# First feed-forward's output part 1 as seven block products, its modulation rows moved, another offset for v's weights

## The chip, the cores and the metric

The kernel runs on one core of a Trainium2 chip. Times are device microseconds of one execution, from three runs per kernel; a profiled execution gives the trace. The core has a tensor engine (PE; PEld is its weight load), a vector engine (DVE), a scalar engine (ACT), GpSimd (POOL) and SyncE (SP), each with an instruction queue of its own that is worked off in order, and 16 DMA engines that SP's and POOL's issues share. Lower is better.

## The reference, cut to what matters

One decoder block for 512 tokens (T) of width 1024 (D), float32. Nine vectors of 1024 come from `c` by one product with `w_ada`; they shift, scale and gate the three sub-layers.

```
mod = silu(c) @ w_ada + b_ada             # sh1 sc1 gt1 sh2 sc2 gt2 sh3 sc3 gt3
u = modulate(rmsnorm(h, g_norm_ffn1), sh1, sc1)
h = h + 0.5 * gt1 * swiglu(u, w_ffn1_in, w_ffn1_out)     # hidden width 2816
u = modulate(rmsnorm(h, g_norm_mix), sh2, sc2)
h = h + gt2 * token_mixing(u, ...)        # pooling mixer and dilated attention, gated
u = modulate(rmsnorm(h, g_norm_ffn2), sh3, sc3)
h = h + 0.5 * gt3 * swiglu(u, w_ffn2_in, w_ffn2_out)
out = rmsnorm(h, g_final)
```

with `swiglu(u, w_in, w_out) = (silu(a) * b) @ w_out`, where `a, b` are the halves of `u @ w_in`.

## The kernel before

**Precision.** Everything is kept transposed (features on partitions, tokens along the free axis). Each float32 operand is split into a high part, which ACT rounds off (`whi`, line 347), and a low part, which DVE takes as the difference (`wlo`, line 359); each product is three matmuls: high by high, high by low, low by high (`mm3`, lines 391 to 393; `product`, 794 to 796; `out_blocks`, 939 to 941).

**Weights.** They come in chunks of 128 by 1024, in the order of a list that `plan` writes. A chunk is loaded by SP (line 267), then split into a ring of about six and a half chunks. `look(4)` emits the splits of the chunks up to four ahead of the one in use. `room` (line 296) places a chunk at an offset of 0 columns modulo 64, or of 16 (`SHIFT`) for those in `shifted`.

**Plain and block products.** A plain chunk is used in 24 matmuls of 512 columns. Elsewhere a two by two block product is formed from seven products of half-size blocks instead of eight: sums of weight blocks (`make`, line 284, on DVE; two more by accumulating DMAs from POOL, line 292), sums of the data blocks, and 24 matmuls of 256 columns for each of seven chunks. `settle` (line 397) is one extra matmul of 240 columns that stands before such a run where the run before it had 512 columns.

**First feed-forward.** The hidden width is 22 tiles of 128. Tiles 0 to 3 are computed in `startup`, 4 and 5 by `ffn_pair`, and from 6 on two at a time by `duo`, which is a block product of seven steps (i = 0 to 6). The output product is cut in five parts (`PARTS`), each placed after the hidden tiles that it needs and two more: parts 0 and 1 plain, 2 and 3 by `out_blocks` (`BLOCK_PARTS`), 4 plain, as the tail. In this order: pairs 4 and 5, part 0, duos 6 and 8, part 1, duos 10 and 12, part 2, duos 14 and 16, part 3, duos 18 and 20, part 4. For a block part the hidden tiles must be combined too: `block_hidden` gives four differences and sums on DVE, and two high and two low parts. `later(n, f)` puts off work by n steps, so that it is emitted behind the splits of that step.

**Banks.** The eight PSUM banks go round by `nb`. `out_blocks` hands them on in the order C, B, A: the duo behind it starts in C[0], which holds output tiles 0 and 1 until `lower(C, 0)` has added them to H on DVE (line 920, emitted at step i = 4).

**Modulation rows.** `mod` is built from 72 rows of `w_ada`, each one DMA (line 410) of 512 KB and one DVE instruction over 1024 columns (line 418) with an accumulated sum. `bg` does the next row and asks for the one after it; from part 0 on the rows alternate between two buffers, `cs` and `AR`. Rows 24 to 44 stand beside the first feed-forward: eight beside part 1 (two of them `later`), four in duo 8 and four in duo 18 (i = 1, 3, 5, 6), five in duo 20 (i = 0 to 4), by the table `ROWS`. The mixer's norm needs rows 24 to 39.

**Mixer's start.** `head` runs the first four projections (q and k of group 0) beside the second half of the norm. Then `rope_a` sends a copy of them across partitions by 16 DMAs on SP (line 1219), and v of group 0 is computed with the token block as the stationary operand and 256 columns of weights as the moving one (lines 1475 to 1477), four blocks of 24 matmuls. Between them stand `rope_b` (lines 1227, 1228) and three rows. Attention scores (line 1265) follow inside the next tile.

**Angles.** `trig` loads the positions by four small DMAs on SP (line 1177) and does 13 short steps, one behind each tile of part 1 and each step of part 2.

Of the kernel before, what the change touches and what calls it, by code (L numbers as in the profile page):

```python
# [11 lines left out]
AF = mybir.ActivationFunctionType  # L12
# [3 lines left out]
T = 512  # L16
# [118 lines left out]
SHIFT = 16  # L135

PLAIN = {0: 6, 2: 4}
PARTS = ((0, 4), (4, 8), (8, 12), (12, 16), (16, 22))
BLOCK_PARTS = {0: (2, 3), 2: (0, 1, 2, 3)}
ROWS = {8: (1, 3, 5, 6), 18: (1, 3, 5, 6), 20: range(5)}  # L140
NH = 6

MERGED = (6, 7, 0, 1, 2, 3, 4, 5)
# [16 lines left out]
class Kernel:  # L160
# [6 lines left out]
    def plan(self):  # L167
# [40 lines left out]
        def shift(i):  # L208

            self.shifted.update(range(len(self.order) - i, len(self.order)))  # L210
# [23 lines left out]
        base = len(self.order)  # L234
# [3 lines left out]
            plain(mx[i + 4:i + 6])  # L238
        plain(mx[-KT:])
        self.shifted.update(range(base, base + 4))  # L240
        shift(3)
        ffn(2, f2i, f2o, 0)
        shift(5)
# [54 lines left out]
    def room(self, i, held):  # L298


        w, u, at, pieces = self.order[i][0], self.unit(i), self.top, []
        shift = SHIFT if i in self.shifted else 0
        at += (shift - at) % 64
        for c in range(0, w, u):
            if at % RING + u > RING:
                at += RING - at % RING + shift
            o = at % RING
            if pieces and pieces[-1][0] + pieces[-1][1].stop - pieces[-1][1].start == o:
                pieces[-1] = (pieces[-1][0], slice(pieces[-1][1].start, c + u))
            else:  # L310
                pieces.append((o, slice(c, c + u)))
            at += u
        low = min((self.start[j] for j in range(held, i)), default=self.top)
        return (pieces, at) if at - low <= RING else None
# [399 lines left out]

    def ffn_post(self, j, s, pb):
        nc = self.nc
        h = self.wk["hf"][:, j % 2 * T:(j % 2 + 1) * T] if self.n else self.work(("hf", "u3")[j % 2], T)
        nc.vector.tensor_tensor(h, s, pb, op=OP.mult)
        if self.n:
            return  # L720
        hh, hl = self.HH[j % NH], self.HL[j % NH]
        nc.scalar.activation(hh, h, AF.Copy)
        nc.vector.tensor_tensor(hl, h, hh, op=OP.subtract)
# [240 lines left out]
    def ffn2(self):  # L964
        self.put, self.now = [], 0
        self.negate(2)
        bk = [self.nb() for _ in range(4)]
        adds, (s2, s1, s0, last) = self.u_steps(2)
        self.head(2, bk, AF.Silu, adds[:3])
        self.todo = [s0[0], adds[3], s0[1], s2[0], adds[4], s2[1], s1[0], adds[5], s1[1]]  # L970
        do = lambda n: [self.todo.pop(0)() for _ in range(n)]
        for j in range(2):
            self.ffn_post(j, self.ffn_silu(j, bk[2 * j]), bk[2 * j + 1])
            do(2)
        late = self.block_hidden(0)
        pa = self.ffn_tile()
        do(3)
        [f() for f in late[:4]]
        do(len(self.todo))
        self.more()  # L980
        [f() for f in late[4:]]
        s, pb = self.ffn_silu(2, pa), self.ffn_tile()
        self.ffn_post(2, s, pb)
        self.ffn_pair(3)
        late = self.block_hidden(2)
        for i, f in zip((1, 1, 1, 1, 3, 3, 4, 4), late):
            self.later(i, f)
        self.ffn(2, 4, lambda: [f() for f in last])

    def negate(self, n):  # L990
        self.minus = self.mod[:, 0:4]
# [31 lines left out]
    def ffn(self, n, j, last=None):  # L1023
# [10 lines left out]
        for part, (k0, k1) in enumerate(PARTS):  # L1034
            tail = part + 1 == len(PARTS)
            extra = 0 if part and part - 1 in BLOCK_PARTS[n] else 1
            while j < pairs_before(n, part):
                if j < PLAIN[n]:
                    self.ffn_pair(j, beside)
                    j += 1  # L1040
                else:
                    self.duo(n, j, last, tail and j + 2 == FT, extra)
                    last, extra = None, 0
                    j += 2
            if n == 0:
                last = self.beside_out(part) or last
# [5 lines left out]
            if not tail:  # L1052
                for m in range(0, KT, 2):
                    self.look(4)
                    w = self.take()
# [56 lines left out]
    def beside_out(self, part):  # L1112

        if part == 0:

            assert not self.adat
            self.ada_pool.close()
            self.ada_free, self.ada_stop = [self.cs, self.AR], 45
            self.bg_fetch()
            self.negate(0)  # L1120
            self.sums = self.open_sums()
            self.todo, last = self.splits[:3], self.splits[3]
            self.ready = False
            self.todo.append(self.more)
            return last
        if part == len(PARTS) - 1:
            assert self.ada_next == 45 and not self.adat, self.ada_next
            self.ada_free = None
            self.retired = self.rawx
            self.free = [b for b in self.free if not any(b is x for x in self.rawx)]  # L1130
            assert not self.todo
            self.trig_spread()
        if part == 1:
            self.todo = self.trig()
# [281 lines left out]
    def mix(self):  # L1416
# [12 lines left out]
        with tc.tile_pool(name="rt", bufs=1) as self.rt, tc.tile_pool(name="aw", bufs=2) as self.aw, \  # L1429
# [15 lines left out]
            nc.sync.dma_start(self.wpool, self.a["wpool"])  # L1445

            bk = [self.nb() for _ in range(4)]
            self.head(1, bk, AF.Exp)

            uf = mp.tile([P, D], F32, name="uc")  # L1450
            self.ada_free, self.ada_stop, self.ada_depth = [self.AR, uf], 58, 2
            self.bg_fetch()

# [11 lines left out]
            w = self.take() + self.take()  # L1465
            self.look(2)
            for n in range(4):
                if n:
                    self.split(self.pos + n - 1)
                    self.fetch()  # L1470
                b = self.nb()
                ts = slice(n * P, n * P + P)
                for k in range(KT):
                    hi, lo = w[k]
                    M(b[:, :256], self.UH[k][:, ts], hi, start=k == 0, stop=False)
                    M(b[:, :256], self.UH[k][:, ts], lo, start=False, stop=False)
                    M(b[:, :256], self.UL[k][:, ts], hi, start=False, stop=k == KT - 1)
                nc.scalar.activation(self.v1[:, n, :], b[:, :256], AF.Copy)
                for i in ((), (0, 1), (2,), (3,))[n]:
                    self.rope_b(*to[i], 1, sw[i])  # L1480
                if n == 1:

                    self.ada_free += [self.v23.rearrange("p n f -> p (n f)")[:, i * D:(i + 1) * D] for i in range(2)]
                if n:
                    self.bg()
                if n == 2:
                    self.ada_free = [t for t in self.ada_free if t is not uf]
# [20 lines left out]
            for g in (1, 2):  # L1508
                for dst in (self.qt[g], self.kt[g]):
                    for hp in range(2):  # L1510
                        b = self.mm_tile(hooks(todo.pop(0), rest + [(7, self.bg)]))
# [15 lines left out]
            b = self.mm_tile(hooks([], rest + [(3, self.bg), (6, lambda: by_class(0)), (7, self.bg)]))  # L1527
# [6 lines left out]
            def half(i):  # L1534
                if not v4:
# [3 lines left out]
            sums, last = self.mix_sums(x + [self.qt[2]], [[wide(ma, "k2"), wide(mp, "uc")],  # L1539
                                       [wide(ma, "v1"), wide(ma, "k0")], [lambda: half(0), lambda: half(1)]])  # L1540
# [427 lines left out]
```

## Time and profile before

| | us |
|---|---|
| median of 3 runs (lowest, highest) | 974.65 (973.73, 975.48) |
| the profiled execution | 975.12 |
| its span in the trace | 973.0 |
| part 1, with its extra matmul behind it (141.02 to 162.91) | 21.89 |
| part 2 (201.00 to 220.04) | 19.04 |
| part 3 (258.12 to 277.17) | 19.05 |
| v of group 0 (372.79 to 384.30) | 11.51 |

The stretches run from the start of a stage's first matmul to the start of the next stage's first one. The mean granted clock of the tensor engine is 0.999. A time in brackets in a row of the timeline is how long the engine stood idle before the instruction, and what ended that; a row with xN merges N instructions.

### The profile page before, as it was taken

The numbers are of one execution on the slowest core, as the hardware profiler recorded it, in microseconds if no ns is written. First come the engines' busy times: TensorE is split into PE (matmuls) and PEld (weight loads), VectorE is DVE, ScalarE is ACT, GpSimd is POOL, SyncE is SP. The second block draws the span as 40 slices with busy tenths as digits, with TensorE's granted clock in tenths as the row PEclk, the third lists the DMA queues.
The fourth block names the chain that finished last, engine by engine and source line by source line (L and its number), as shares of the span: only waits on it lengthen the run. The fifth ranks groups of instructions, "written<-read, shape, count | busy, mean of one in ns | idle before, by whom it ended". The sixth has DMA issues, their size and how long they took to land.

```text
span 973.0 us, 17631 instructions
## 1 busy us (share of the span) xinstructions
PE 964.1 (99%) x7115; PEld 898.8 (92%) x7115; DVE 824.4 (85%) x1190; ACT 524.8 (54%) x784; POOL 69.7 (7%) x77
## 2 busy tenths in 40 slices
PE   9999999999999999999999999999999999999997
PEld 7888998999999899878879998998999999999997
DVE  7989989999899776898888877889899888989663
ACT  5443553674755453445645553465666657555553
POOL 0000100101010000006300000000101100110002
PEclk9999999999999999999999999999999999999999
DMA  9857777776668525665143327713757666666512
GB/s 351 281 179 254 203 250 217 222 200 155 180 166 266 167 58 183 222 191 179 40 141 109 108 66 224 251 51 111 188 149 187 168 169 173 165 161 153 162 33 87
DMA packets 51507, 165.94 MB, mean 171 GB/s; under 512 B 7009, under 2 KB 9825, under 8 KB 51426
## 3 DMA queue, kind: packets, MB, share of 16 engines
q1 hardware_dynamic: 44224, 140.18, 44.2%
q0 software_dynamic: 6624, 24.12, 14.0%
q8 instruction: 55, 0.90, 0.4%
q10 hardware_dynamic: 578, 0.53, 0.2%
q14 instruction: 26, 0.21, 0.1%
HBM read 135.29 MB, written 2.24 MB: 141 GB/s over the span
## 4 chain that ended last, share of the span: by engine, by line
PE 94%; DVE 3%; issue 1%; DMA 1%; ACT 1%; POOL 0%; POOLq 0%; SPq 0%; DVEq 0%
PE bank L796 13%; PE bank L795 13%; PE bank L794 13%; PE bank L391 11%; PE bank L392 11%; PE bank L393 11%; PE bank L941 4%; PE bank L940 4%; PE bank L939 4%; PE bank L1894 2%; PE bank L1896 1%; PE bank L1898 1%; PE bank L1563 1%; PE bank L1265 1%; PE bank L1316 1%
## 5 line engine op out<-in xcount | busy, mean ns | idle before, releaser
L359 DVE TENSOR_TENSOR wlo<-raw,whi 128x1024 fp32r<-128x1024 f32 (+3 forms) x156 | 169.2, 1095 | 40.9 <-ACT whi L347 40.7
L794 PE MATMUL bank<-UH,whi 128*128 128x256 f32 x640 | 176.7, 276 | 0.0
L795 PE MATMUL bank<-UL,whi 128*128 128x256 f32 x640 | 176.7, 276 | 0.0
L796 PE MATMUL bank<-UH,wlo 128*128 128x256 f32 x640 | 176.7, 276 | 0.0
L359 DVE TENSOR_TENSOR wlo<-X,whi 128x1024 fp32r<-128x1024 f32 (+3 forms) x123 | 135.6, 1112 | 22.6 <-ACT whi L347 22.0
L347 ACT ACTIVATE whi<-raw 128x1024 fp32r<-128x1024 f32 (+3 forms) x156 | 143.9, 938 | 18.2 <-DVE raw L284 10.5
L347 ACT ACTIVATE whi<-X 128x1024 fp32r<-128x1024 f32 (+3 forms) x123 | 117.1, 969 | 22.4 <-DVE X L284 17.0
L794 PEld LDWEIGHTS bank<-UH,whi 128*128 128x128 f32 x640 | 120.1, 188 | 0.2
L795 PEld LDWEIGHTS bank<-UL,whi 128*128 128x128 f32 x640 | 120.1, 188 | 0.0
L796 PEld LDWEIGHTS bank<-UH,wlo 128*128 128x128 f32 x640 | 120.1, 188 | 0.0
L796 PE MATMUL bank<-SH,wlo 128*128 128x256 f32 x408 | 112.6, 276 | 0.0
L794 PE MATMUL bank<-SH,whi 128*128 128x256 f32 x408 | 112.6, 276 | 0.0
L795 PE MATMUL bank<-SL,whi 128*128 128x256 f32 x408 | 112.6, 276 | 0.0
L391 PE MATMUL bank<-UH,whi 128*128 128x512 f32 (+1 forms) x304 | 105.9, 348 | 0.0
L392 PE MATMUL bank<-UL,whi 128*128 128x512 f32 (+1 forms) x304 | 104.5, 344 | 0.0
L393 PE MATMUL bank<-UH,wlo 128*128 128x512 f32 (+1 forms) x304 | 104.3, 343 | 0.0
L795 PEld LDWEIGHTS bank<-SL,whi 128*128 128x128 f32 x408 | 76.6, 188 | 0.0
L796 PEld LDWEIGHTS bank<-SH,wlo 128*128 128x128 f32 x408 | 76.6, 188 | 0.0
L794 PEld LDWEIGHTS bank<-SH,whi 128*128 128x128 f32 x408 | 76.6, 188 | 0.0
L391 PE MATMUL bank<-HI,whi 128*128 128x512 f32 (+1 forms) x214 | 71.5, 334 | 0.0
L392 PE MATMUL bank<-HK,whi 128*128 128x512 f32 (+1 forms) x214 | 71.1, 332 | 0.0
L393 PE MATMUL bank<-HI,wlo 128*128 128x512 f32 (+1 forms) x214 | 71.1, 332 | 0.0
(373 smaller groups left out, 2290.8 us busy)
## 6 DMA issues: line engine op xcount, KB each, us to landing
raw<-wmix SPq DMA_DIRECT2D x44, 512.0 KB, 3.9
raw<-wf1i SPq DMA_DIRECT2D x32, 512.0 KB, 4.8
raw<-wf2i SPq DMA_DIRECT2D x30, 512.0 KB, 4.3
ada<-wada SPq DMA_DIRECT2D x23, 512.0 KB, 5.6
X<-raw POOLq DMA_DIRECT2D x22, 512.0 KB, 5.3
AR<-wada SPq DMA_DIRECT2D x17, 512.0 KB, 4.5
X<-wf2i SPq DMA_DIRECT2D x14, 512.0 KB, 4.8
cs<-wada SPq DMA_DIRECT2D x11, 512.0 KB, 4.4
```

The source lines that it names most:

```text
L347: self.nc.scalar.activation(self.hi[:, y], r[:, x], AF.Copy)
L359: self.nc.vector.tensor_tensor(self.lo[:, y], r[:, x], self.hi[:, y], op=OP.subtract)
L391: M(ps, hi, uh, start=start, stop=False)
L392: M(ps, hi, ul, start=False, stop=False)
L393: M(ps, lo, uh, start=False, stop=stop)
L794: M(o, hi, uh, start=start and p == 0 and k == 0, stop=False, skip_group_check=True)
L795: M(o, hi, ul, start=False, stop=False, skip_group_check=True)
L796: M(o, lo, uh, start=False, stop=k == 3, skip_group_check=True)
L939: M(o, hi, uh, start=start and m % 2 == 0 and k == 0, stop=False, skip_group_check=True)
L940: M(o, hi, ul, start=False, stop=False, skip_group_check=True)
L941: M(o, lo, uh, start=False, stop=k == 1, skip_group_check=True)
L1894: M(b, hi, self.UH[k], start=k == 0, stop=False)
```

## The change

Part 1 of the first feed-forward's output is done by `out_blocks`. Its hidden tiles 4 and 5, which come from plain pairs, are therefore kept whole (`ffn_post` returns early for them) and combined by `block_later`, emitted beside part 0. The rows are placed anew: none beside part 1; i = 3 and 6 in duos 8, 12 and 16; five in duo 18; five in duo 20; and five (40 to 44) in the mixer's `head`, with buffers `uc`, `q1`, `k1` and then `AR`. The two chunks of v's weights get offset 48, and a `settle` matmul stands before v's first block.

```diff
-BLOCK_PARTS = {0: (2, 3), 2: (0, 1, 2, 3)}
-ROWS = {8: (1, 3, 5, 6), 18: (1, 3, 5, 6), 20: range(5)}
+BLOCK_PARTS = {0: (1, 2, 3), 2: (0, 1, 2, 3)}
+ROWS = {8: (3, 6), 12: (3, 6), 16: (3, 6), 18: (0, 1, 3, 5, 6), 20: range(5)}
...
         self.shifted.update(range(base, base + 4))
+        self.beside = range(base + 4, base + 6)
...
-        shift = SHIFT if i in self.shifted else 0
+        shift = 3 * SHIFT if i in self.beside else SHIFT if i in self.shifted else 0
...
-        h = self.wk["hf"][:, j % 2 * T:(j % 2 + 1) * T] if self.n else self.work(("hf", "u3")[j % 2], T)
+        whole = j >= PLAIN[0] - 2 or self.n
+        h = self.wk["hf"][:, j % 2 * T:(j % 2 + 1) * T] if whole else self.work(("hf", "u3")[j % 2], T)
         nc.vector.tensor_tensor(h, s, pb, op=OP.mult)
-        if self.n:
+        if whole:
             return
...
-        late = self.block_hidden(2)
-        for i, f in zip((1, 1, 1, 1, 3, 3, 4, 4), late):
-            self.later(i, f)
+        self.block_later(2)
         self.ffn(2, 4, lambda: [f() for f in last])
+
+    def block_later(self, j):
+        for i, f in zip((1, 1, 1, 1, 3, 3, 4, 4), self.block_hidden(j)):
+            self.later(i, f)
...
                     self.ffn_pair(j, beside)
                     j += 1
+                    if j == PLAIN[0]:
+                        self.block_later(j - 2)
...
-            self.ada_free, self.ada_stop = [self.cs, self.AR], 45
+            self.ada_free, self.ada_stop = [self.cs, self.AR], 40
...
-            self.head(1, bk, AF.Exp)
-
             uf = mp.tile([P, D], F32, name="uc")
+            self.ada_free, self.ada_stop, self.ada_depth = [uf, self.qt[1], self.kt[1]], 45, 3
+            self.bg_fetch()
+            self.ada_free.append(self.AR)
+            self.head(1, bk, AF.Exp, [self.bg] * 5)
+            assert self.ada_next == 45 and not self.adat, self.ada_next
             self.ada_free, self.ada_stop, self.ada_depth = [self.AR, uf], 58, 2
             self.bg_fetch()
...
                 ts = slice(n * P, n * P + P)
+                if n == 0:
+                    self.settle(b, self.UH[0][:, ts], w[0][0])
                 for k in range(KT):
```

More of the change, by code (lines that the diff above doesn't have):

```diff
@@ L984, in ffn2 @@
         self.ffn_pair(3)
-        late = self.block_hidden(2)
-        for i, f in zip((1, 1, 1, 1, 3, 3, 4, 4), late):
+        self.block_later(2)
+        self.ffn(2, 4, lambda: [f() for f in last])
+    def block_later(self, j):
+        for i, f in zip((1, 1, 1, 1, 3, 3, 4, 4), self.block_hidden(j)):
             self.later(i, f)
-        self.ffn(2, 4, lambda: [f() for f in last])
     def negate(self, n):
@@ L1126, in beside_out @@
         if part == len(PARTS) - 1:
-            assert self.ada_next == 45 and not self.adat, self.ada_next
+            assert self.ada_next == 40 and not self.adat, self.ada_next
             self.ada_free = None
```

## The prediction

> **What bounds the kernel.** I read the page's engine shares, then the chain that ended last, then the busy time of each engine stage by stage.
>
> ```profile
> PE 964.1 (99%) x7115; PEld 898.8 (92%) x7115; DVE 824.4 (85%) x1190; ACT 524.8 (54%) x784; POOL 69.7 (7%) x77
> PE 94%; DVE 3%; issue 1%; DMA 1%; ACT 1%; POOL 0%; POOLq 0%; SPq 0%; DVEq 0%
> 102.82:141.02 38.20, 38.20 (x339) 38.20 (x337) 32.52 (x38) 23.21 (x32) 2.61 (x3) 1.00 0.81 229
> 141.02:162.91 21.89, 21.89 (x99) 18.13 (x98) 19.94 (x33) 7.36 (x8) 0.87 (x1) 1.00 0.71 219
> 162.91:201.00 38.09, 38.09 (x338) 38.09 (x337) 37.28 (x49) 20.89 (x28) 4.33 (x5) 1.00 0.80 226
> 201.00:220.04 19.04, 19.04 (x170) 19.04 (x169) 17.16 (x24) 15.30 (x24) 0.95 (x2) 1.00 0.75 201
> 258.12:277.17 19.05, 19.05 (x171) 19.05 (x170) 16.06 (x19) 13.58 (x19) 1.72 (x2) 1.00 0.68 168
> 277.17:315.25 38.08, 38.08 (x339) 38.08 (x337) 36.30 (x52) 19.33 (x27) 1.75 (x2) 1.00 0.77 232
> 356.06:372.55 16.49, 16.49 (x142) 16.49 (x141) 8.98 (x18) 6.44 (x12) 0.00 (x0) 1.00 0.37 128
> 372.90:384.30 11.40, 11.40 (x97) 11.40 (x96) 9.26 (x14) 5.60 (x10) 0.00 (x0) 1.00 0.44 97
> ```
>
> In the stretches the columns are length, then PE, PEld, DVE, ACT and POOL busy, clock, DMA share and GB/s. PE is never idle at full clock, so the time is the number of matmuls times their spacing. Two things then decide: what PE no longer does, and whether DVE (83 to 98% busy in the same stretches) stays far enough ahead.
>
> **The change part by part.** *Part 1.* It goes from the 96 wide matmuls and one `settle` of the second stretch (21.89) to 168 narrow ones as in part 2 (19.04, 113.3 ns each): 21.89 − 19.04 = 2.85 us less, settle included, since duo 10 now follows 256-column products as duo 14 does.
>
> *Work for DVE.* A 1024-column instruction holds DVE 1.14 us when packed (312.85 to 314.00 below); shorter ones from these groups (busy, mean ns, idle):
>
> ```profile
> L418 DVE SCALAR_TENSOR_TENSOR cs<-cs,cond 128x1024 f32<-128x1024 f32 x11 | 13.4, 1218 | 0.3 <-DMA cs<-wada 0.3
> L889 DVE TENSOR_TENSOR GK<-wide,GI 128x768 fp32r<-128x768 f32 x4 | 3.8, 953 | 0.0
> L887 DVE SCALAR_TENSOR_TENSOR wide<-wide 128x256 f32<-128x256 f32 x8 | 3.4, 425 | 0.3
> 80.79 0.69 DVE L723 TENSOR_TENSOR HK<-wide,HI 128x512 fp32r<-128x512 f32 x1 [0.70 <-ACT HI L722]
> 90.20 0.69 DVE L723 TENSOR_TENSOR HK<-ev,HI 128x512 fp32r<-128x512 f32 x1 [0.70 <-ACT HI L722]
> 125.73 1.23 DVE L359 TENSOR_TENSOR wlo<-X,whi 128x1024 fp32r<-128x1024 f32 x1 [2.32 <-ACT whi L347]
> 126.88 1.22 DVE L819 TENSOR_TENSOR wide<-wide 128x1024 f32<-128x1024 f32 x1
> 137.14 1.29 DVE L359 TENSOR_TENSOR wlo<-X,whi 128x768 fp32r<-128x768 f32 x2 [1.00 <-ACT whi L347]
> 141.24 1.22 DVE L418 SCALAR_TENSOR_TENSOR AR<-AR,cond 128x1024 f32<-128x1024 f32 x1
> 142.87 1.94 SPq L1177 DMA_DIRECT2D tr<-pos  x4
> 149.03 0.23 DVE L1181 CAST tr<-tr 128x128 f32<-128x128 int32 x1 [1.14 <-DMA tr<-pos]
> 216.76 1.66 DVE L920 SCALAR_TENSOR_TENSOR H<-bank,mod,H 128x256 f32<-128x256 f32 x4
> ```
>
> Beside part 0, `block_hidden(4)` adds 4 × 0.4 + 1.14 + 0.87 = 3.6 us; the two L723 fall away with their waits on ACT, 2 × (0.60 + 0.70) = 2.6, and some 0.3 of waits of the splits behind them. So nothing there, and the 2.32 us idle before 125.73 covers the rest.
>
> From 126.88 on, up to the start of part 1: two rows fewer (−2.3), block sums and G of tiles 6 and 7 (+1.6 + 0.9), two `make` for part 1 (+2.3), less 1 us of idle (137.14): DVE reaches the end of its last row before part 1 some 1.3 us later, at 143.7 instead of 142.4. Behind that row SP sends a row's DMA and then the four of `trig`: 144.2 to 146.1 instead of 142.87 to 144.81. They landed 4.2 us after issue (cast at 149.03), so they bound the cast to 150.3 at the most; DVE itself arrives at 148.3 (one half-width add, a split, a multiply and the four block sums: 0.6 + 1.14 + 1.2 + 1.6). Between the cast and the second update of `lower(C, 0)`, which frees C[0], stand seven 1024-column instructions, GK, five small steps and two updates: 8.0 + 0.9 + 0.8 + 0.8 = 10.5. C[0] is free at 158.8 to 160.8; duo 10 wants it at 141.02 + 19.04 = 160.06. In part 2 this had 2.4 us to spare (216.76 + 0.8 against 220.04). I take 0 for this stall (the lower end, as there are fewer loads in flight than before); its upper end is 2 us, with the scatter of my sum.
>
> *Rows in duos 12 and 16.* One and two more rows; parts 2 and 3 have 1.9 and 3.0 us of idle DVE (19.04 − 17.16, 19.05 − 16.06) to take them: 0.
>
> *Rows in duos 18 and 20.* One more, and the closing steps of row 39 move from duo 18 to the end of duo 20. There DVE's lag does cost:
>
> ```profile
> 297.97 0.17 DVE L429 TENSOR_TENSOR mod<-mod,vecs 128x8 f32<-128x8 f32 x1
> 306.14 0.33 SPq L410 DMA_DIRECT2D AR<-wada  x1
> 310.66 1.23 DVE L418 SCALAR_TENSOR_TENSOR AR<-AR,cond 128x1024 f32<-128x1024 f32 x1 [1.40 <-DMA AR<-wada]
> 312.85 1.23 DVE L418 SCALAR_TENSOR_TENSOR cs<-cs,cond 128x1024 f32<-128x1024 f32 x1
> 314.00 0.95 DVE L359 TENSOR_TENSOR wlo<-raw,whi 128x768 fp32r<-128x768 f32 x1
> 315.45 0.60 ACT L816 ACTIVATE wide<-bank 128x512 f32<-128x512 f32 x1 [2.98 <-PE bank L796]
> 317.13 1.22 DVE L819 TENSOR_TENSOR wide<-wide 128x1024 f32<-128x1024 f32 x1
> 319.48 1.23 DVE L826 TENSOR_TENSOR HK<-wide,HI 128x1024 fp32r<-128x1024 f32 x1 [1.13 <-ACT HI L801]
> 320.94 0.40 PE L392 MATMUL bank<-HK,whi 128*128 128x512 f32 x1
> ```
>
> The last product's silu is ready at 316.05, but DVE multiplies only at 317.13, then come the high part on ACT and the low part, done at 320.7: 0.24 us before PE wants it. The new row at i = 0 of duo 18 puts DVE 1.14 us back, with no idle until the row loads; 0.25 is absorbed there (0.3 idle in the `cs` group above). The 1.40 us of idle before 310.66 absorbs nothing, because that row's load goes out only after the row before in the same buffer (306.14), which is late too. With the closing steps (0.4, lines 429 and 431) the multiply is 0.9 + 0.4 = 1.3 late, so PE waits 1.3 − 0.24 = 1.05. Bounds: 0 if the loads land sooner, 1.6 if DVE gets nothing back. I take 0.9.
>
> *Mixer's head and v.*
>
> ```profile
> AR<-wada SPq DMA_DIRECT2D x17, 512.0 KB, 4.5
> 366.84 0.42 SPq L410 DMA_DIRECT2D uc<-wada  x1
> 366.92 0.48 DVE L529 SCALAR_TENSOR_TENSOR UL<-ev,mod,UH 128x256 fp32r<-128x256 f32 x1 [0.18 <-ACT UH L515]
> 372.70 4.99 SPq L1219 DMA_DIRECT2D q<-v  x8
> 372.71 1.29 DVE L1221 TENSOR_TENSOR q<-bank,cs 128x512 f32<-128x512 f32 x2 [5.31 <-ACT v L1216]
> 377.23 1.22 DVE L359 TENSOR_TENSOR wlo<-raw,whi 128x1024 fp32r<-128x1024 f32 x1 [2.04 <-ACT whi L347]
> 387.70 0.69 DVE L1228 TENSOR_TENSOR k<-k,k 128x512 f32<-128x512 f32 x1
> 387.82 1.12 PE L1265 MATMUL bank<-k,q 64*128 64x128 f32 x8
> ```
>
> One row fits ahead of the norm's last steps, four into the 5.31 us of idle before 372.71 (4 × 1.14 = 4.6). The last waits for a load that can leave only about when uc's left before (366.84) and lands some 4.5 us later (the first row, median), at 371.3, and SP's 16 copies stand behind the next loads into the same buffers. Cost 0 to 1 us; I take 0.1. v's 96 matmuls go from 11.51/96 = 120 ns to perhaps 113.3, less one settle of 0.11: −0.53 of PE. But the scores at 387.82 wait for DVE's last rope step (387.70 + 0.69), and DVE is packed from 377.23, whose start hangs on the end of v's first block, which moves by 0.05 only. I take −0.05; bounds −0.53 and 0.
>
> Sum: −2.85 + 0 + 0 + 0.9 + 0.1 − 0.05 = −1.9 us. Profiled, 975.12 − 1.9 = 973.2; the median of the runs lies 0.47 under the profiled execution: 974.65 − 1.9 = **972.75**, say 972.7.
>
> ```profile
> L939 PEld LDWEIGHTS bank<-HI,whi 128*128 128x128 f32 x192 | 36.0, 188 | 0.0
> ```
>
> A weight load is 188 ns here and yet narrow matmuls follow every 113 ns, so loads are hidden. The Trainium skill, page "TensorE: Matmul & The Clock Gate", section "Back-to-back issue gap", gives sustained spacings of about 81 ns at 128 columns and 131 at 512, where a load and matmul pair has a large fixed share. By its line an estimate for 256 is 98, and part 1 would go from 96 × 131 = 12.6 to 168 × 98 = 16.4, 3.8 us slower. The trace disagrees (227 and 113 ns, near proportional).
>
> **The rivals.** *All covers hold (A).* The tail's row loads land early and DVE keeps up: −2.85 − 0.05, 971.7. For: 4 us landings vary by a microsecond or two, and one microsecond suffices. Against: the fixed order of buffers.
>
> *C[0] is late too (B).* The bank computed above comes 0.5 to 2 us late: 973.2 to 974.7, centre 974. For: DVE's demand in duos 6, 8 and part 1 is about their length. Against: 2.4 us spare in part 2.
>
> *A stall that leaves PE out of step, slower (C).* The place is duo 10's first product, the price a slower spacing of everything behind it. In the head, after a wait, 140 matmuls of 256 took 16.49 us (117.8 ns each) with nothing to set them right. If C[0] comes after 160.06 and the same step sets in, six duos and two parts (8 × 168 = 1344 matmuls) lose 4.5 ns each, 6.0 us, since no settle stands there any more: 972.7 + 0.5 + 6.0 = 979, or 976 and up if the step comes back midway. Against: it needs B first, and parts 2 and 3 run without it.
>
> *Loads not hidden (D).* If each narrow matmul took its load's 188 ns, part 1 would last 168 × 0.188 = 31.6, +9.7: 984. Parts 2 and 3 speak against it. The Trainium skill's rule quoted above leans towards it.
>
> *v does nothing.* The offset leaves 120 ns: the time is the forecast's within 0.1, as DVE sets that point.
>
> **How the numbers follow.** Forecast (972.2 to 973.2, v's case within it) 0.43, A 0.27, B 0.17, C 0.11, D 0.02. 0.2% of 974.65 is 1.95 us, about what can be told from no change. Faster (under 972.7): A 0.27 and some 0.17 of the forecast, 0.44. Slower (over 976.6): C, D and a remainder of the stalls adding up, 0.15. Within: 0.41. The range leaves out C and D and a little of A: 971.3 to 975.2; the forecast's own is 972.2 to 973.2.
>
> **What would show it.** Part 1 at 19.04 from first matmul to duo 10's first (more is B); spacing in duos 10 to 20 at 113.3 (118 is C); no gap at the second half of the tail's first two tiles, HK ready before PE's L392 (a gap is the 0.9); v's stretch near 11.0, and the wait among the eight scores longer by as much. I am wrong if part 1 saves less than 2.8, or if PE waits in places not named, such as part 0 or the norm's second half.

## The result, and the profile after

The changed kernel takes 981.27 us (median of 9 runs, 975.76 to 982.87) against 974.93 (9 runs, 973.73 to 976.57): a ratio of 1.0057, 95% interval 1.0035 to 1.0078. It is slower by 6.3 us, where 972.7 was forecast. Its runs also lie much further apart than those of before: 7 us against 3. The profiled execution is one of the shortest, 976.68 us (span 974.9); it shows a first part of the loss (its span is 1.9 us longer than before), and the other runs must hold more.

The page of the profiled execution, engine shares and then the chain that ended last:

```profile
PE 961.5 (99%) x7187; PEld 898.8 (92%) x7187; DVE 838.2 (86%) x1222; ACT 534.3 (55%) x806; POOL 70.3 (7%) x79
...
PE 82%; DVE 9%; DMA 3%; issue 3%; ACT 1%; SPq 1%; POOL 0%; POOLq 0%; DVEq 0%; ACTq 0%
```

PE is busy 2.6 us less than before, but the chain now runs 9% through DVE and 3% through DMA (before 3% and 1%): there are waits of PE that these end. Where, by stretches (columns as in the prediction: part 1; duos 10 and 12; duos 14 to 20 with part 3; the tail; v):

```profile
141.29:160.33 19.04, 19.04 (x170) 19.04 (x169) 17.95 (x29) 13.36 (x19) 1.12 (x2) 1.00 0.77 212
160.33:198.85 38.52, 38.36 (x338) 38.16 (x337) 36.38 (x48) 21.90 (x29) 3.57 (x5) 1.00 0.64 166
217.89:313.09 95.20, 95.20 (x842) 95.20 (x841) 90.12 (x117) 54.92 (x75) 7.78 (x9) 1.00 0.74 209
313.09:331.78 18.69, 16.95 (x74) 13.44 (x73) 14.74 (x21) 8.48 (x12) 0.00 (x0) 1.00 0.51 145
372.42:383.31 10.89, 10.89 (x99) 10.89 (x97) 8.02 (x12) 5.54 (x9) 0.00 (x0) 1.00 0.59 174
```

Part 1 is 19.04, as forecast. The next stretch is 0.43 longer than 38.09, and the tail is 18.69 where before it is 16.39:

```profile
315.25:331.64 16.39, 16.39 (x74) 13.51 (x73) 12.46 (x15) 8.48 (x12) 0.00 (x0) 1.00 0.50 142
```

By the starts of the same matmuls in the two traces (v after by its new settle), the difference after − before runs like this:

| at the start of | before | after | difference | change |
|---|---|---|---|---|
| pairs | 59.30 | 59.57 | +0.27 | |
| duo 10 | 162.91 | 160.33 | −2.58 | −2.85 |
| part 2 | 201.00 | 198.85 | −2.15 | +0.43 |
| tail | 315.25 | 313.09 | −2.16 | −0.01 |
| settle behind the tail | 331.64 | 331.78 | +0.14 | +2.30 |
| v | 372.79 | 372.30 | −0.49 | −0.63 |
| mixer tile behind v | 384.30 | 383.31 | −0.99 | −0.50 |
| last scores of that tile | 388.45 | 388.89 | +0.44 | +1.43 |
| second settle in front of the last norm | 941.74 | 943.05 | +1.31 | +0.87 |
| end of the span | 973.0 | 974.9 | +1.9 | +0.6 |

The 0.43 in duo 12, in the timeline of ACT and PE:

```profile
181.60 1.06 ACT L348 ACTIVATE whi<-raw 128x1024 fp32r<-128x1024 f32 x1 [1.43 <-DMA raw<-X]
...
189.93 0.59 ACT L803 ACTIVATE ev<-bank 128x512 f32<-128x512 f32 x1
...
190.57 0.39 PE L796 MATMUL bank<-SH,whi 128*128 128x256 f32 x1 [0.16 <-ACT ev L803]
```

ACT stands idle until an accumulating DMA of POOL has landed; everything behind that split in its queue is late, last the copy that hands a bank back to PE. POOL issues this DMA only behind a `make` of DVE: 13.98 us after duo 10's first matmul (174.31 − 160.33), where before it was 12.79 (175.70 − 162.91). The 2.30 in the tail:

```profile
310.01 1.23 DVE L419 SCALAR_TENSOR_TENSOR cs<-cs,cond 128x1024 f32<-128x1024 f32 x1 [1.63 <-DMA cs<-wada]
...
312.62 1.23 DVE L419 SCALAR_TENSOR_TENSOR AR<-AR,cond 128x1024 f32<-128x1024 f32 x1 [0.50 <-DMA AR<-wada]
...
317.33 1.23 DVE L821 TENSOR_TENSOR wide<-wide 128x1024 f32<-128x1024 f32 x1
...
318.59 1.06 ACT L803 ACTIVATE HI<-wide 128x1024 fp32r<-128x1024 f32 x1 [4.70 <-DVE wide L821]
...
319.70 0.50 PE L392 MATMUL bank<-HI,whi 128*128 128x512 f32 x1 [0.98 <-ACT HI L803]
...
320.95 0.50 PE L393 MATMUL bank<-HK,whi 128*128 128x512 f32 x1 [0.76 <-DVE HK L828]
```

DVE's multiply (line 821, was 819) starts 4.24 us behind the tail's first matmul; before it was 1.88 (317.13 − 315.25). By the clock it starts at nearly the same time (317.33 against 317.13): PE has come 2.16 us earlier, DVE has not. The last two rows of duo 20 wait 1.63 and 0.50 for their loads, and the closing steps follow. And the 1.43 among the scores:

```profile
371.01 0.33 SPq L411 DMA_DIRECT2D AR<-wada  x1
...
372.16 0.33 SPq L411 DMA_DIRECT2D uc<-wada  x1
...
372.58 6.05 SPq L1225 DMA_DIRECT2D q<-v  x8
...
378.70 0.69 DVE L1233 TENSOR_TENSOR q<-q,cs 128x512 f32<-128x512 f32 x1 [0.76 <-DMA q<-v]
...
381.53 1.22 DVE L419 SCALAR_TENSOR_TENSOR AR<-AR,cond 128x1024 f32<-128x1024 f32 x1
...
385.14 1.22 DVE L419 SCALAR_TENSOR_TENSOR uc<-uc,cond 128x1024 f32<-128x1024 f32 x1
...
388.89 0.49 PE L1271 MATMUL bank<-k,q 64*128 64x128 f32 x4 [1.58 <-DVE k L1234]
```

PE reaches the scores a microsecond earlier than before (386.81 against 387.82; the head runs at 113 ns a matmul in its second half, v at 113), but DVE's rope chain ends 0.4 later than it did: two row loads stand ahead of SP's copies, and DVE waits 0.76 for the first copies. All that PE gained is waited away.

### The profile page after: what moved, and what is told of

Same layout as the page of the kernel before. It is cut to its first block, busy times and chain, and to the rows that moved or that the text cites. A ratio compares the mean times of both kernels' runs of the same rounds, so it can differ in the third digit from the quotient of the medians.

```text
span 974.9 us, 17849 instructions
## 1 busy us (share of the span) xinstructions
PE 961.5 (99%) x7187; PEld 898.8 (92%) x7187; DVE 838.2 (86%) x1222; ACT 534.3 (55%) x806; POOL 70.3 (7%) x79
## 4 chain that ended last, share of the span: by engine, by line
PE 82%; DVE 9%; DMA 3%; issue 3%; ACT 1%; SPq 1%; POOL 0%; POOLq 0%; DVEq 0%; ACTq 0%
PE bank L796 10%; PE bank L798 10%; PE bank L797 10%; PE bank L392 10%; PE bank L393 10%; PE bank L394 10%; PE bank L942 4%; PE bank L941 4%; PE bank L943 4%; DVE wlo L360 3%; PE bank L1905 2%; PE bank L1909 1%; PE bank L1907 1%; DMA AR<-wada 1%; DVE H L922 1%
## 5 line engine op out<-in xcount | busy, mean ns | idle before, releaser
L360 DVE TENSOR_TENSOR wlo<-raw,whi 128x1024 fp32r<-128x1024 f32 (+6 forms) x157 | 170.1, 1094 | 38.1 <-ACT whi L348 38.0
L348 ACT ACTIVATE whi<-raw 128x1024 fp32r<-128x1024 f32 (+6 forms) x157 | 144.1, 934 | 31.9 <-DVE raw L285 10.4
L360 DVE TENSOR_TENSOR wlo<-X,whi 128x1024 fp32r<-128x1024 f32 (+6 forms) x136 | 140.0, 1044 | 17.6 <-ACT whi L348 17.4
L348 ACT ACTIVATE whi<-X 128x1024 fp32r<-128x1024 f32 (+6 forms) x136 | 121.3, 915 | 36.0 <-DVE X L285 29.5
L796 PEld LDWEIGHTS bank<-UH,whi 128*128 128x128 f32 x640 | 120.1, 188 | 0.2
L797 PEld LDWEIGHTS bank<-UL,whi 128*128 128x128 f32 x640 | 120.1, 188 | 0.0
L798 PEld LDWEIGHTS bank<-UH,wlo 128*128 128x128 f32 x640 | 120.1, 188 | 0.0
L392 PEld LDWEIGHTS bank<-UH,whi 128*128 128x128 f32 x304 | 57.1, 188 | 8.6 <-issue 1.9
L394 PEld LDWEIGHTS bank<-UH,wlo 128*128 128x128 f32 x304 | 57.1, 188 | 7.0
L393 PEld LDWEIGHTS bank<-UL,whi 128*128 128x128 f32 x304 | 57.1, 188 | 6.8 <-DVE UL L530 0.3
```

What stands on the lines that cost most here:

```text
L348: self.nc.scalar.activation(self.hi[:, y], r[:, x], AF.Copy)
L360: self.nc.vector.tensor_tensor(self.lo[:, y], r[:, x], self.hi[:, y], op=OP.subtract)
L392: M(ps, hi, uh, start=start, stop=False)
L393: M(ps, hi, ul, start=False, stop=False)
L394: M(ps, lo, uh, start=False, stop=stop)
L796: M(o, hi, uh, start=start and p == 0 and k == 0, stop=False, skip_group_check=True)
```

## The experiments

Lines of diffs are against the changed kernel, if nothing else is said. All of these kernels compute the whole block. PE is called in step where its 256-column matmuls follow each other every 113.3 ns, and out of step where they follow every 117.8; it loses the step when it goes from the first to the second.

**e1: the changed kernel once more.** No edit.

> The changed kernel once more, to catch the profile of an execution that takes 981 to 983 us rather than 976.7. Out of step (rival C): two or more duos between 160 and 313 us show a spacing near 118 ns in place of 113.3, so that the stretch from the first matmul of duo 10 to the tail's first one is 157 to 159 us against 152.8 in the profile of 976.7, while part 1 stays at 19.0. More waits (the rival): the spacing stays at 113.3 and single gaps of PE, of 0.4 us and more, in duos 10 to 20, in the tail and in the mixer add up to the 5 to 6 us.

979.54 us (979.39 to 981.74; before on that chip 974.53), profiled at 979.39. Two places differ from the shorter profile. First duo 10, DVE, ACT and PE:

```profile
164.97 1.28 DVE L931 TENSOR_TENSOR ev<-ev,bank 128x512 f32<-128x512 f32 x2
...
165.74 0.58 ACT L803 ACTIVATE bank<-bank 128x512 f32<-128x512 f32 x1 [2.71 <-DVE ev L931]
...
166.37 0.19 PEld L796 LDWEIGHTS bank<-SH,whi 128*128 128x128 f32 x1 [0.28 <-ACT bank L803]
```

C[0] came 0.1 us late at duo 10's first product, PE then ran 46 matmuls at 118 ns, and at the third product it waited for a second bank: DVE's sums of the block part (line 931) release it. Behind this wait it was in step again, up to the tail, so the lost step cost this execution 0.2 us. Part 1 itself took 19.20 here (141.18 to 160.38): PE waited in its middle too, behind a copy of ACT. Then the tail, PE's timeline and, below it, the busy times of the stretch behind these waits:

```profile
321.02 0.50 PE L392 MATMUL bank<-HI,whi 128*128 128x512 f32 x1 [2.02 <-ACT HI L803]
322.28 0.50 PE L393 MATMUL bank<-HK,whi 128*128 128x512 f32 x1 [0.76 <-DVE HK L828]
```

```profile
322.85:326.50 3.65, 3.65 (x10) 2.81 (x9) 1.86 (x3) 0.63 (x1) 0.00 (x0) 0.53 0.03 11
```

The granted clock of the stretch is 0.53: nine 512-column matmuls take 3.65 us instead of 2.04. So there is a third loss that neither theory had: PE waits, and then runs at half clock, 1.6 us more. This execution lost its time in waits (2.02 and 0.76 in the tail, 2.26 at the scores) and in that stretch.

**e2: a settle ahead of duos 10, 14 and 18.**

```diff
-            extra = 0 if part and part - 1 in BLOCK_PARTS[n] else 1
+            extra = 0 if n and part and part - 1 in BLOCK_PARTS[n] else 1
```

> One settle matmul ahead of duos 10, 14 and 18 (3 x 0.11 us). If the 981 to 983 us come from duos that run out of step behind a block part, all runs fall to 976 to 977. If the step is lost at another place, or the time goes into waits, the median stays at 980 to 982.

980.62 us (978.75 to 984.51): no better. The settle did not keep PE in step, it put it out of step: in its profile the matmuls behind the settle of duo 10 start every 118 ns at once, and after a wait in that duo they stay at 118 up to duo 18. There the third settle found the step again, so such a matmul can do either.

**e3: the row of duo 18 elsewhere.**

```diff
-ROWS = {8: (3, 6), 12: (3, 6), 16: (3, 6), 18: (0, 1, 3, 5, 6), 20: range(5)}
+ROWS = {6: (4,), 8: (3, 6), 12: (3, 6), 16: (3, 6), 18: (1, 3, 5, 6), 20: range(5)}
```

> The row at i = 0 of duo 18 goes to i = 4 of duo 6. If that row is what makes the tail's HK late, the two gaps of the tail (together 2.3 us in the profile of the changed kernel) shrink to 0.2 to 0.5 us and the time falls by about 2 us. If the closing steps behind the last row and its late loads do it, they stay above 1.5 us and the time does not move.

977.21 us (973.45 to 985.04). The tail, in the stretch from its first matmul to the settle:

```profile
317.84:334.59 16.75, 16.69 (x75) 13.44 (x73) 12.86 (x17) 8.49 (x12) 0.00 (x0) 1.00 0.45 136
```

0.36 above before's 16.39, where the changed kernel had 2.30. The median is 2.3 us below e1's on the same chip, with runs from 973 to 985. But this profile lost the step in duo 12 and ran 1078 matmuls at 117.8 ns, 4.9 us: PE came that much later to the tail, which gives DVE time, so the 0.36 is not the row's doing alone. e5 and e8 below both reach the tail in step, e5 (first) with this row and e8 without it:

```profile
312.28:332.57 20.29, 16.91 (x74) 13.45 (x73) 15.21 (x21) 8.56 (x13) 0.00 (x0) 1.00 0.52 157
```

```profile
312.38:329.70 17.32, 16.66 (x74) 13.44 (x73) 13.47 (x17) 8.48 (x12) 0.00 (x0) 1.00 0.48 131
```

So the row makes most of the tail's loss, and 0.93 us stays without it (17.32 − 16.39).

**e4: the kernel before with v's offset and settle alone** (the three edits of the change that concern v).

> The kernel before with v's offset and settle alone. v's 96 matmuls go from 11.5 to 10.9 us. If DVE's rope steps set the scores, as in the prediction, the wait among the scores grows by the same 0.6 and the time stays within 0.1 us of before; if PE sets them, the time falls by 0.5 to 0.6 us. It does not touch the first feed-forward, so its runs should not scatter more than those of before.

975.12 us (973.95 to 976.85), ratio 1.0006 (0.9997 to 1.0016). v is 0.6 shorter, and the last scores start 0.91 us behind the ones in front of them instead of 0.41: DVE sets them, as predicted.

**e5: the angles one part later.**

```diff
-        if part == 1:
+        if part == 2:
             self.todo = self.trig()
```

> The steps of the angles stand beside parts 2 and 3 in place of 1 and 2: some 1.7 us less for DVE (the wait for their DMA and five short steps) ahead of the two releases that duo 10 waits for. If DVE's lag behind part 1 makes PE stumble in duos 10 and 12 and fall out of step there, C[0] and the sums come over a microsecond early, duos 10 to 20 run at 113.3 ns and the time falls by 2 to 4 us, to 976 to 977, with the tail's and the scores' waits left. If the stumbles come from the late accumulating DMA in duo 12 or from elsewhere, the median stays at 979 to 982.

979.73 us (978.94 to 980.05). In the profile duos 10 and 12 take 38.08 us with no gap, so DVE's lag behind part 1 was the cause there (POOL's DMA goes out 12.84 us behind duo 10's first matmul, 172.60 − 159.76, near the 12.79 of the kernel before); but PE then waited 2.62 + 0.76 us in the tail and 2.46 at the scores, with one half-clock stretch: DVE's chain ends no earlier for it (PE goes on in the tail at 320.5, in the two profiles of the changed kernel at 319.7 and 321.0), and what PE gains ahead is waited away. The time was missed for that reason.

**e6: part 1 plain again,** the rest of the change kept, no rows beside part 1.

> Part 1 plain again, and no rows beside it: the new places of the rows, the head's five rows and v's offset remain. If the block product of part 1 is what puts DVE late, there is no stumble in duos 10 and 12, all runs lie together, and part 1 takes 21.9 us again: 2.85 us more than the block part, less the steps lost: 977 to 979. If the rows in duos 8 and 12 do it, the stumbles are still there and the runs scatter from 979 to 985. The tail's gaps and the scores' wait stay in both cases.

979.69 us (979.09 to 981.24). Duos 10 and 12 run without a gap, with the same rows in duos 8 and 12: it is the block product that puts DVE late there. And without any gain in part 1 the rows, the head and v cost 5.1 us by themselves, with no step lost in the profile: waits of 0.66 + 0.77 us in the tail (18.33 long in all, 1.94 more than before), 2.38 at the scores, and a half-clock stretch.

**e7: two rows out of the rope chain.**

```diff
-                if n:
+                if n > 2:
                     self.bg()
-                if n == 2:
-                    self.ada_free = [t for t in self.ada_free if t is not uf]
...
-            self.ada_free, self.ada_stop, self.ada_depth = [self.AR, uf], 58, 2
+            self.ada_free, self.ada_stop, self.ada_depth = [self.AR], 57, 2
...
-                        b = self.mm_tile(hooks(todo.pop(0), rest + [(7, self.bg)]))
+                        b = self.mm_tile(hooks(todo.pop(0), rest + [(2, self.bg)] * (len(todo) == 6) + [(7, self.bg)]))
...
-            beside = [(1, 7, nxt), (2, 2, nxt), (2, 3, clear), (2, 6, self.bg), (2, 7, nxt), (3, 2, self.at_swap), (3, 2, nxt),
+            beside = [(0, 7, self.bg), (1, 7, nxt), (2, 2, nxt), (2, 3, clear), (2, 6, self.bg), (2, 7, nxt), (3, 2, self.at_swap), (3, 2, nxt),
```

> Rows 45 and 46 leave the chain of rope steps beside v for later stages of the mixer (two instructions of 1.14 us, and one load less ahead of SP's copies). If DVE's chain sets the scores, PE's wait of 1.6 to 2.3 us there falls to 0 to 0.4, and with it the half-clock stretch that follows waits of about 2 us: 1.6 to 3.5 us off the median, 976 to 978. If the copies' DMAs set it, the wait falls by no more than 0.5 us.

978.98 us (977.32 to 982.36): the median missed, the mechanism not. The eight scores run without a wait (PE, timeline):

```profile
391.85 0.71 PE L1271 MATMUL bank<-k,q 64*128 64x128 f32 x8
```

But two duos of the first feed-forward take 39.58 us instead of 38.08 (stretch):

```profile
220.32:259.90 39.58, 39.58 (x339) 39.58 (x337) 35.88 (x44) 20.79 (x28) 3.44 (x4) 1.00 0.68 177
```

PE is busy all through at full clock, and each matmul takes 117.8 ns. This execution lost the step at 166 us, at the wait for the second bank (0.37 us in all; C[0] was in time), and kept it lost until the tail: 1294 × 4.5 ns = 5.8 us. Its first feed-forward is that of the changed kernel, line for line.

**e8: e3, e5 and e7 together.**

> The three edits together: angles one part later, the row of duo 18 in duo 6, two rows out of the rope chain. If the three waits are independent, part 1's 2.85 us and some 1 us of v and the head come through: 970 to 971.5, in all runs. If one wait only hands over to another, 973 to 976, and scattered.

973.76 us (971.71 to 978.83; before 974.57), 0.9998 (0.9982 to 1.0014). Between the two theories: no gap between pair 4 and the tail, none at the scores, 0.9 in the tail; but two runs at 978 to 979, and 1.25 us of waiting in the mixer behind the row moved there.

**e9 and e10: more rows moved.** e9 takes the last row of duo 20 to i = 5 of duo 12, and the mixer's row from (0, 7) to (0, 1); e10 also takes a row of duo 8 to pair 5.

> The three edits of before and two more: the last row of duo 20 goes to i = 5 of duo 12, and the row that held up the copy of the third class (PE idle 1.25 us there) goes to the idle stretch ahead of it. If the tail's remaining gap hangs on that row's load, it falls from 0.7 us to 0.2 or less; with the copy on time another 1 us goes: 971 to 972 for the bulk of the runs. If the tail's gap stays, it is the closing steps and the split behind them.

> As e9, and the second row of duo 8 goes ahead of part 0, to pair 5, where DVE has 3 us of idle time: 1.1 us more slack for the two releases that duo 10 waits for. If the runs at 978 in e8 come from a stumble there, all runs lie within 971 to 972.5; if they come from elsewhere, some are still 5 us longer than the rest.

e9: 975.05 us (970.65 to 979.91); e10: 973.96 (971.67 to 975.68; before 974.87), 0.9987 (0.9978 to 0.9997). In both the mixer's wait grew, to 1.84, and the row in duo 12 made part 2's banks late; e9's tail kept its 0.76. e10's profile shows what is left of the scatter, against e8 at the same place in duo 8 (ACT):

```profile
131.18 1.07 ACT L348 ACTIVATE whi<-X 128x1024 fp32r<-128x1024 f32 x1 [2.80 <-DMA X<-raw]
...
133.83 0.57 ACT L803 ACTIVATE ev<-bank 128x512 f32<-128x512 f32 x1
```

```profile
128.32 1.06 ACT L348 ACTIVATE whi<-X 128x1024 fp32r<-128x1024 f32 x1
...
130.98 0.57 ACT L803 ACTIVATE ev<-bank 128x512 f32<-128x512 f32 x1
```

The same accumulating DMA lets the split start 2.9 us later, and the copy that frees PE's bank stands behind it. POOL issued it at nearly the same time in both (122.42 in e8, 122.58 in e10).

**e11: the waits of the changed kernel filled** with matmuls of no use, four in the tail and seven ahead of the scores.

> The changed kernel with idle time of PE filled: four 512-column matmuls of no use in the tail's gap and seven in the wait among the scores, 0.9 and 1.6 us, about what PE waits there at the least. If the half-clock stretches follow from PE standing idle some 2 us, none is left, the granted clock is 0.999 in all runs, and the median falls by 1 to 2 us to 978 to 980. If they have another cause, the clock stays at 0.995 to 0.997 in most runs and the time does not fall.

981.95 us (977.11 to 984.31). No half-clock stretch in its profile (clock 0.998), and other runs had 0.995 and 0.997. On the half clock it is inconclusive; e13 and e14 were made for that. But its profile shows rival C. Up to the tail this kernel is the changed one; C[0] came 0.2 us late at duo 10's first product, and PE was out of step from there to the tail (stretch):

```profile
161.66:320.40 158.74, 158.67 (x1346) 158.47 (x1346) 146.06 (x193) 90.87 (x127) 13.03 (x15) 1.00 0.71 194
```

The changed kernel's profile of 976.68 has 152.76 for this stretch. The 6.0 us between them are the spacing: 1340 × 4.5 ns.

**e12: the kernel before with one settle ahead of duo 14.**

```diff
-                    self.duo(n, j, last, tail and j + 2 == FT, extra)
+                    self.duo(n, j, last, tail and j + 2 == FT, 1 if n == 0 and j == 14 else extra)
```

> The kernel before with one settle matmul ahead of duo 14, where 256-column matmuls follow 256-column ones: no wait, no other work, 0.11 us by itself. If a shift of PE by a part of a matmul is enough to put the pairs of matmul and weight load out of step for good, duo 14 to duo 20 run at 117.8 instead of 113.3 ns: 840 x 4.5 ns = 3.8 us, 978.3. If only a true wait does it, or the step is found again, the time stays at 974.6 to 975.

978.24 us (977.93 to 979.72; before 974.87): to 0.1 us what was expected of the loss of step. Duos 14 and 16, then part 3:

```profile
219.86:259.43 39.57, 39.57 (x339) 39.57 (x337) 35.38 (x44) 20.65 (x28) 4.13 (x5) 1.00 0.66 165
259.43:279.22 19.79, 19.79 (x171) 19.79 (x169) 16.31 (x19) 13.57 (x19) 1.72 (x2) 1.00 0.65 162
```

No engine is late here and PE never stands idle. One matmul of another length is enough, and here nothing sets PE right until 512-column matmuls come.

**e13 and e14: the kernel before with one or two DVE instructions of no use in the rope chain** (one in the diff; two in its place in e14).

```diff
+                for _ in range(1 if n == 3 else 0):
+                    nc.vector.tensor_tensor(self.ev[:, :D], self.ev[:, D:], self.ev[:, D:], op=OP.add)
                 for i in ((), (0, 1), (2,), (3,))[n]:
```

> The kernel before with one DVE instruction of 1.14 us and of no use in the rope chain ahead of the scores, so that PE's wait there grows from 0.4 to about 1.5 us. If the half-clock stretch needs about 2 us of idle time, none comes: the time rises by 1.1 us, to 975.9, and the granted clock stays at 0.998 to 0.999. If any wait of PE over 1 us brings it on, the time rises by 2.7 us.

> Two such instructions: a wait of about 2.7 us. If standing idle for more than 2 us halves PE's clock for one stretch of 3.4 us, the time rises by 2.3 + 1.7 = 4.0 us, to 978.8, the clock falls to 0.997, and the trace shows some eight 512-column matmuls of 427 ns behind the wait. If the half-clock stretches of the changed kernel had another cause, it rises by 2.3 us, to 977.1, at 0.999.

e13: 975.98 us (975.35 to 976.94), clock 0.998 to 0.999 in all ten runs. e14: 977.10 (976.84 to 978.75), and here the two theories share the runs: three at 976.8 to 977.1 with clock 0.999, two at 978.4 and 978.8 with 0.997 and 0.996. One of these was profiled; e13's wait, then e14's wait, and the stretch behind e14's:

```profile
389.47 0.49 PE L1265 MATMUL bank<-k,q 64*128 64x128 f32 x4 [1.27 <-DVE k L1228]
```

```profile
390.48 0.56 PE L1265 MATMUL bank<-k,q 64*128 64x128 f32 x4 [2.53 <-DVE k L1228]
```

```profile
390.97:394.39 3.42, 3.42 (x11) 2.70 (x9) 3.32 (x15) 0.83 (x5) 0.00 (x0) 0.53 0.92 316
```

So a wait of 2.5 us brings the half clock on in some executions, at 1.6 us each, and one of 1.3 in none.

**e15: the rest of DVE's work out of the way.** As e10, with the row of duo 12 in pair 5 too and the mixer's row in the third gate tile.

> As e10, with the row of duo 12 in pair 5 as well and the last row of the mixer's classes in the third gate tile, away from GpSimd's work. If DVE's lag and its collision with GpSimd were what the earlier versions lost, the wait of 1.84 us at the class copy and the gaps at duo 14 go: 970.5 to 972 for most runs. If late accumulating DMAs (4.9 us in one execution, 7.6 in another) still make PE stumble in some duo, the runs scatter from 971 to 975 as before.

972.21 us (970.84 to 979.71; before 974.40), 0.9984 (0.9967 to 1.0000). Ten of the twelve runs are at 970.8 to 973.7, two at 978.7 and 979.7, with clock 0.998 and 0.999.

**e16: e12 with a 512-column matmul ahead of its settle. e17: such pairs ahead of duos 12 and 16 in e15.**

```diff
         if extra:
+            if extra > 1:
+                M(bank, w[0][0], self.UH[0], start=True, stop=True, skip_group_check=True)
             self.settle(bank, w[0][0], self.UH[0])
...
-                    self.duo(n, j, last, tail and j + 2 == FT, extra)
+                    self.duo(n, j, last, tail and j + 2 == FT, 2 if n == 0 and j == 14 else extra)
```

(In e17 `j in (12, 16)` stands for `j == 14`.)

> As e12, with one 512-column matmul of no use ahead of the settle: 0.23 + 0.11 us. If the settle is right behind 512-column matmuls and wrong behind 256-column ones, duos 14 to 20 run at 113.3 ns again and the time is that of before and 0.34, 974.7 to 974.9. If any matmul put in there loses the step, it is 978 as in e12.

> e15 with such a pair (512 columns, then the settle) ahead of duos 12 and 16, 0.7 us. If e15's two runs at 979 are executions that lost the step in duos 8 to 14, it is found again at the next pair, and no run is more than 2 us above the median of 972.5 to 973. If they lost time elsewhere, single runs still lie at 978 to 980.

e16: 975.25 us (974.38 to 977.38; before 974.80), 1.0005 (0.9992 to 1.0017): duos 14 and 16 take 38.09 again. e17: **972.82 us** (971.68 to 974.31 in twelve runs; before 974.80), 0.9975 (0.9964 to 0.9985), and no long run. Twelve runs are too few to say that they are gone: e15 had two in twelve, and of the kernel before one run in 23 on this chip took 980.42, with clock 0.999. Its profiled execution happened to lose the step in duo 6; the stretch out of step and the one behind the pair, then the pair itself (PE):

```profile
119.73:162.02 42.29, 42.29 (x361) 42.29 (x360) 40.87 (x53) 28.93 (x40) 4.54 (x6) 1.00 0.76 209
182.63:201.22 18.59, 18.59 (x167) 18.59 (x165) 17.33 (x21) 11.38 (x15) 1.74 (x2) 1.00 0.64 182
```

```profile
181.80 0.40 PE L792 MATMUL bank<-UH,whi 128*128 128x512 f32 x1
182.04 0.27 PE L398 MATMUL bank<-UH,whi 128*128 128x240 f32 x1
```

42.29 us for 359 starts is 117.8 ns; 18.59 for 164 is 113.4. The extra matmuls found the step again.

## Why the prediction was wrong

**Part 1 saves 2.85: right,** to the hundredth, in the profile of 976.68 (162.91 − 141.02 against 160.33 − 141.29). Not in every execution: waits in its middle made it 19.20 in e1 and 20.16 in e11.

**C[0] at duo 10, taken as 0: the step that failed first.** The wait itself was within its bounds (0 in the first profile, 0.1 in e1, 0.2 in e11). But a second release of the same part, DVE's sums, was not looked at (0.35 in e1), and the price does not lie in the wait. Rival C had mechanism and size: it said 6.0 us, 979; e11 shows 6.0, e7 5.8 from the second release on, e12 the same 4.5 ns per matmul. Its chance, 0.11, rested on "it needs B first", a C[0] late by 0.5 us or more. It does not: a wait of 0.1 to 0.4 us at a product of a duo can do it (seen in duos 6, 10, 12 and 14), in some executions, and in e12 no wait at all. The changed kernel's own two profiles lost the step for 46 matmuls at the most; that its long runs lost it for longer is inferred from e7 and e11. (A slip on the way: the terms of DVE's lag ahead of part 1 add up to 1.5 us, not 1.3. And DVE is 54 to 98% busy in the stretches shown there, not 83 to 98%; the low ones are the head and v.)

**Rows in duos 12 and 16 at 0:** their cover was read as DVE's idle time. By e6 the rows are indeed harmless beside a plain part 1; by e5 and e6, one profile each, the 0.43 us in duo 12 is the block part's lag.

**The tail, 0.9 with bounds 0 and 1.6: right mechanism, wrong size.** 2.30 us, and 1.94 in e6, where PE comes no earlier. The row at i = 0 of duo 18 makes most of it (e5 against e8, 0.93 left). The sum had DVE's multiply 1.3 us late; it was 2.36, because both last loads were late, not the first alone: each goes out only when DVE has emptied its buffer, and takes its four to five microseconds from there.

**Head 0.1 and v −0.05:** together +0.30 in the profile of 976.68, within the bounds, for the reason given (e4, e7). In other profiles PE waits longer at the scores (2.26 in e1; 2.38 in e6, and there the half clock follows). The head's spacing falling from 118 to 113 ns in these executions was not foreseen, and worth nothing, since DVE sets the scores.

**Not in the working at all:** the 0.87 us in the mixer's classes (a stage of its pooling; below) and the half clock, 1.6 us each time. It turns PE's waits into more than their length, and the change makes two of them, in the tail and at the scores, long enough. How much this and the waits come to is seen in e6: 5.1 us without the block product and without a lost step in the profile.

For the profiled execution the span should have been 1.9 us shorter and was 1.9 longer: 1.4 more in the tail, 0.43 in duo 12, 0.25 at head, v and scores, 0.87 in the classes, 0.27 and 0.6 at start and end. The other 4.6 us up to the median are put down to longer waits as in e1, half-clock stretches and lost steps (5.8 and 6.0 in e7 and e11). How the unprofiled runs divide between them is not recorded, beyond their clock. The run of 982.46 us has 0.999, so a half-clock stretch cannot explain it, and a lost step would. Two runs have 0.995 and 0.996, lower than any profile here without such a stretch; at 0.997 (three more) it cannot be told, since e7's profile has 0.997 without one: its last 5 us, behind its last matmul, are at half clock.

Rival A needed loads early by a microsecond; they were late. Rival B was too small: in none of the three profiles named was C[0] late by its 0.5 us. Rival D fell: part 1's narrow matmuls keep 113.3 ns. The case "v does nothing" fell too: its spacing did change, and DVE swallowed it.

## What to carry to other kernels

Where PE is the bound, a stage in front of a wait that another engine ends is worth nothing by itself: first look up what ends the next waits, and move that work. Price a wait by what it leaves behind: whether the matmuls after it are spaced as before, and whether it is long enough to cost the clock. Look for every release that the next stage needs, not the first alone; and where executions differ, profile more than one.

## What the runs showed of the hardware

**A lost step lasts.** 256-column matmuls run at 113.3 or at 117.8 ns with full clock and no idle time, and change from one to the other at a wait or at one odd matmul. A 240-column matmul right behind 512-column ones keeps the faster spacing (before, e16); behind 256-column ones it can lose it (e2, e12) or find it again (e2, at duo 18).

**Half clock behind a wait.** In six profiles (e1, e2, e3, e5, e6, e14) a stretch of 3.41 us at half clock followed waits of 1.96 to 2.53 us; none followed 1.27, 1.58 or 1.84, and none two long ones, 2.62 in e5's tail and 2.26 at e1's scores. It depends on where the wait falls. The clock changes on a grid: in e1 it is full for 317.44 us, half for 3.41 and full for 648.53, which is 93, 1 and 190 times 3.413, and the other profiles give whole multiples too. Cut by each execution's grid, the six had 1.86 to 2.53 us of idle time within the one window ahead of the slow one; the 2.62 was split into 1.94 and the rest, the 2.26 into 1.02 and 1.24. So a limit lies near 1.9 us within one window, no sharper than that. The Trainium skill, page "TensorE: Matmul & The Clock Gate", section "What's actually happening", says that the clock goes to half after an idle window of about 3.4 us that runs freely, and that the windows are of that length. The length of the slow stretches and the grid agree here; the idle time that is needed is shorter than a window.

**DVE against GpSimd.** In the mixer's classes two splits (line 360, was 359) met GpSimd's adds. After, DVE and POOL, and PE's wait for it; then the same two engines before:

```profile
457.94 3.96 DVE L360 TENSOR_TENSOR wlo<-raw,whi 128x1024 fp32r<-128x1024 f32 x2 [2.69 <-ACT whi L348]
...
458.89 5.31 POOL L1395 TENSOR_TENSOR rt<-rt 128x525 f32<-128x525 f32 x3
...
459.94 0.51 PE L1575 MATMUL bank<-wlo,uc 128*128 128x512 f32 x1 [0.42 <-DVE wlo L360]
```

```profile
456.57 2.38 DVE L359 TENSOR_TENSOR wlo<-raw,whi 128x1024 fp32r<-128x1024 f32 x2 [2.69 <-ACT whi L347]
...
456.62 1.26 POOL L1397 TENSOR_TENSOR k<-rt,cst 64x16 f32<-64x16 f32 x1
457.95 2.16 POOL L1398 TENSOR_TENSOR k<-k,tr 64x512 f32<-64x512 f32 x1
```

Before, GpSimd was the one that was held up (1.26 us for an add that takes 0.22 elsewhere); after, DVE was (1.98 each instead of 1.19), since the two had shifted by two microseconds against each other (DVE's splits start 1.37 later, the same small add of GpSimd 0.71 earlier, 455.91 against 456.62). The Trainium skill, page "SBUF — State Buffer", section "SBUF: two separate sides", says that the two share a port pair that is held by one instruction at a time; this agrees. No run here took the collision away by itself.
